# A four-layer decoder trunk on one Trainium2 core: program order and hand plan replaced by a list scheduler; layer 3's queries in 512-column products, its sinks as a score column, norm sums on GpSimd

## The chip, the core and the metric

The kernel runs on one core of one Trainium2 chip. The core has five engines that run their own instruction queues in order: PE (TensorE, matrix products), DVE (VectorE), ACT (ScalarE), POOL (GpSimd) and SP (SyncE, which here only issues DMAs). The metric is the time of one execution in device microseconds. The kernel before takes 1160.29 us (median of three runs, 1159.99 to 1162.09).

## What is computed

256 tokens of width 1024 pass through four layers, all in fp32. Cut to what matters:

```python
for i in range(4):
    a = rms_norm(h, attn_norm_g[i])
    # i % 3 == 0: differential attention (layers 1 and 4), 8 heads of 2x64, values of 128
    # i % 3 == 1: block attention, plain causal at 256 tokens (layer 2), 16 heads of 64
    # i % 3 == 2: window of 128, 16 query heads over 2 key heads, biases and sinks (layer 3)
    h = h + mixer(a) @ w_out
    u = max(rms_norm(h, mlp_norm_g[i]) @ w_up, 0)          # 1024 -> 4096
    h = h + (u * u) @ w_down
return rms_norm(h, final_norm_g)

# layer 3, one head: s are the masked scores, sink is one number per head
m = max(max(s, -1), sink)
p = exp(s - m) / (sum(exp(s - m)) + exp(sink - m))
```

In layers 1 and 4 the difference of two softmaxes is taken and its product with the values is normed again, head by head.

## The kernel before

**Numbers in two parts.** Every operand of a large product is split into a high and a low part in PE's fast fp32 format, and each product is made of three: high by high, high by low, low by high. A product of 128 weight columns with 256 tokens is written as one 512-column instruction (high weights by both token parts) and one 256-column instruction (low weights by the high part). Where the tokens are the stationary side (`proj`, `p_last`) it is three instructions of the width of the weight piece.

**Weights.** They are streamed from HBM in 193 DMAs, nearly all 1 MB pieces of 128x2048. ACT makes the high part of each piece in two halves (`whi`, L80) and DVE the low part (`wlo`, L81). Four raw pieces and three split ones fit in SBUF.

**Stages of a layer.** `proj` makes queries, keys and values (PE tiles `p_in`). The norm's factor r is not needed before these leave PSUM: the gain alone is put on the activations (`hg`), and r is a column factor at the eviction. Its sum of squares is made as squares on ACT (`sq`, L231) and sums on DVE (`acc`, L236 and L240), summed across partitions by a product with ones on PE (`p_sum`, L247), and turned into r by ten small DVE instructions (`rsqrt`, L205 to L209). Evictions then go to `qk`, `v` or `qn`, rotary terms are put on (L302 to L307), PE turns queries and keys (`p_qk`, L454), `scores` (PE `p_s`, DVE L331, ACT exponentials) and `transposed` (`p_t`) follow, the product with the values (`p_av`) gives `oo`, and the output product (`p_d`, `p_e`) adds to the residual stream `hT`. Then `up_proj` (16 groups, `p_up`) and `down_proj` (8 groups, `p_down`); in the last layer `down_out` makes the token-major `p_last` and the final norm. In the feed-forward the norm's factor is a row of 256 numbers (`p_row`, L262).

**The joint of two layers** is the place where the last group of `down_proj` is added to `hT`, its gain and square made, the sum over partitions taken and r found, while PE already runs the next layer's first `p_in` products. r has to be there when PE comes to the first `p_qk`, which stands behind 73 instructions of `p_in` in layers 2 and 4.

**What sets the order.** The program is written in the order of the work. Inside layers 1, 2 and 4 a hand-written plan (L558 to L561) says behind which half of which `proj` each block of attention goes; in layer 3 a three-deep line of heads (`step`, L436) does. The Tile framework then sets the order on each engine from this. In layer 3, queries come in four 256-column products of four heads' pairs each, and each head's sink enters as an extra exponential on ACT (`es`, L338) and an addition on DVE (`l`, L339). In layers 1 and 4 each pair of heads runs the ten-step `rsqrt` on DVE between its values and `o` (L402). PSUM's eight banks are four of `wk` (short work) and four of `acc` (sums).

## Time and profile before

| what | value |
| --- | --- |
| median of three runs | 1160.29 us |
| profiled execution | span 1158.7 us |
| instructions | 16976 |
| PE busy | 1140.8 us, 98% |
| PE weight load busy | 980.9 us, 85% |
| DVE busy | 832.8 us, 72% |
| ACT busy | 663.7 us, 57% |
| POOL busy | 11.4 us, 1% |
| DMA, mean of the span | 171 GB/s |

The profiled execution's own time is its span, 1158.7 us, and some 1.6 us lie between that and the median of the runs; a sum made against the span is carried to the median by adding 1.6. A matmul's record lasts longer than the pitch at which they follow one another, since they are pipelined, so PE's busy share cannot be read as the share of useful work. A row of a timeline gives start, length, engine, line, operation and tiles; a row of the waits gives the engine that waited, for whom, how long in all and how often.

### The profile page before, as it was taken

How to read it: one execution, taken by the hardware profiler on the slowest of the kernel's cores; microseconds unless marked ns; L12 is line 12 of the kernel's file. 1: busy time of each engine (PE TensorE's matmuls, PEld its weight loads, DVE VectorE, ACT ScalarE, POOL GpSimd, SP SyncE). 2: the span in 40 equal slices, each digit the busy share in tenths (PEclk: the TensorE clock that was granted, in tenths of full speed). 3: DMA queues.
4: the chain of work that ended last, by engine and by line, in shares of the span. 5: the costliest groups of instructions: out<-in, count | busy, mean ns of one | idle time of the engine just before them, and what ended most of it. 6: DMA issues, size and time to landing. Idle time of an engine off the chain costs nothing.

```text
span 1158.7 us, 16976 instructions
## 1 busy us (share of the span) xinstructions
PE 1140.8 (98%) x6484; PEld 980.9 (85%) x6484; DVE 832.8 (72%) x1672; ACT 663.7 (57%) x1213; POOL 11.4 (1%) x39
## 2 busy tenths in 40 slices
PE   9999999999999999999999999999999999999996
PEld 7788888888887788888899688888888889888885
DVE  7887977656676697775669798775567788777453
ACT  6876656544476666654446665654447676655341
POOL 1000000000000000000000000000000000000000
PEclk9999999999999999999999999999999999999998
DMA  9543465555544355555553245555553444554540
GB/s 330 188 145 111 164 203 193 200 185 184 180 146 146 114 178 202 199 182 186 190 213 127 73 146 190 199 193 182 185 198 132 153 151 141 194 194 163 194 169 37
DMA packets 30321, 198.66 MB, mean 171 GB/s; under 512 B 3488, under 2 KB 4640, under 8 KB 7072
## 3 DMA queue, kind: packets, MB, share of 16 engines
q1 hardware_dynamic: 29952, 197.06, 49.3%
q8 instruction: 51, 0.84, 0.3%
q10 hardware_dynamic: 288, 0.52, 0.1%
q14 instruction: 30, 0.25, 0.1%
HBM read 196.52 MB, written 1.05 MB: 171 GB/s over the span
## 4 chain that ended last, share of the span: by engine, by line
PE 89%; DVE 6%; ACT 2%; DMA 1%; issue 1%; SPq 0%; ACTq 0%
PE p_up L591 20%; PE p_in L294 15%; PE p_down L591 15%; PE p_up L592 10%; PE p_down L592 8%; PE p_last L270 2%; PE p_last L269 2%; PE p_last L271 2%; DVE wlo L81 2%; PE p_e L591 1%; PE p_t L349 1%; PE p_d L591 1%; PE p_s L269 1%; DMA raw<-in_weights 1%; PE p_av L429 1%
## 5 line engine op out<-in xcount | busy, mean ns | idle before, releaser
L81 DVE TENSOR_TENSOR wlo<-raw,whi 128x1024 fp32r<-128x1024 f32 (+1 forms) x374 | 447.3, 1209 | 203.3 <-ACT whi L80 202.8
L80 ACT ACTIVATE whi<-raw 128x1024 fp32r<-128x1024 f32 (+1 forms) x374 | 384.2, 1045 | 211.9 <-issue 109.8
L591 PE MATMUL p_up<-hg,whi 128*128 128x512 f32 x1024 | 356.8, 393 | 0.2
L592 PE MATMUL p_up<-hg,wlo 128*128 128x256 f32 x1024 | 285.2, 279 | 0.0
L591 PE MATMUL p_down<-uu,whi 128*128 128x512 f32 x768 | 266.4, 392 | 0.0
L591 PEld LDWEIGHTS p_up<-hg,whi 128*128 128x128 f32 x1024 | 191.6, 187 | 43.3 <-DVE hg L227 0.7
L592 PE MATMUL p_down<-uu,wlo 128*128 128x256 f32 x768 | 214.3, 279 | 0.0
L294 PE MATMUL p_in<-whi,hg 128*128 128x512 f32 (+1 forms) x736 | 212.5, 371 | 0.3 <-ACT whi L80 0.2
L592 PEld LDWEIGHTS p_up<-hg,wlo 128*128 128x128 f32 x1024 | 193.2, 189 | 0.4
L591 PEld LDWEIGHTS p_down<-uu,whi 128*128 128x128 f32 x768 | 143.7, 187 | 32.2
L294 PEld LDWEIGHTS p_in<-whi,hg 128*128 128x128 f32 x736 | 132.1, 188 | 23.5 <-ACT whi L80 1.3
L592 PEld LDWEIGHTS p_down<-uu,wlo 128*128 128x128 f32 x768 | 144.8, 188 | 0.0
L294 PE MATMUL p_in<-wlo,hg 128*128 128x512 f32 (+1 forms) x368 | 129.9, 368 | 0.2 <-DVE wlo L81 0.2
L664 ACT ACTIVATE uu<-u 128x512 fp32r<-128x512 f32 x64 | 40.5, 633 | 72.2 <-DVE u L662 72.2
L294 PEld LDWEIGHTS p_in<-wlo,hg 128*128 128x128 f32 x368 | 68.8, 189 | 11.7 <-DVE wlo L81 0.8
L597 ACT ACTIVATE cross<-p_up 128x256 f32<-128x256 f32 x128 | 48.2, 376 | 39.6 <-PE p_up L592 34.8
L226 ACT ACTIVATE hg<-hT,gn 128x256 fp32r<-128x256 f32 x64 | 31.7, 502 | 66.4 <-DVE hT L610 65.0
L334 ACT ACTIVATE e<-ns,nm 128x128 f32<-128x128 f32 (+1 forms) x128 | 56.9, 446 | 11.0 <-DVE nm L331 10.3
L665 DVE TENSOR_TENSOR uu<-u,uu 128x512 fp32r<-128x512 f32 x64 | 44.2, 691 | 21.8 <-ACT uu L664 21.8
L598 DVE TENSOR_TENSOR relu<-p_up,cross 128x256 f32<-128x256 f32 x128 | 53.5, 418 | 1.4 <-ACT cross L597 1.3
L271 PE MATMUL p_last<-whi,uu 128*128 128x512 f32 x128 | 49.8, 389 | 0.0
L270 PE MATMUL p_last<-wlo,uu 128*128 128x512 f32 x128 | 49.8, 389 | 0.0
(181 smaller groups left out, 1245.1 us busy)
## 6 DMA issues: line engine op xcount, KB each, us to landing
raw<-in_weights SPq DMA_DIRECT2D x181, 1024.0 KB, 4.9
raw<-in_weights SPq DMA_DIRECT2D x8, 256.0 KB, 4.5
raw<-in_weights SPq DMA_DIRECT2D x4, 512.0 KB, 8.1
hT<-in_xT SPq DMA_DIRECT2D x8, 128.0 KB, 4.3
bias<-in_swa_row SPq DMA_DIRECT2D x1, 512.0 KB, 3.5
grow<-in_fng SPq DMA_DIRECT2D x1, 512.0 KB, 3.7
out<-res ACTq DMA_DIRECT2D x2, 256.0 KB, 2.7
out<-res SPq DMA_DIRECT2D x2, 256.0 KB, 2.7
```

The lines of the kernel that those rows point to most:

```text
L80: A.activation(hi[:, s], raw[:, s], AF.Copy)
L81: V.tensor_tensor(lo[:, s], raw[:, s], f(hi[:, s]), op=OP.subtract)
L270: T.matmul(out, lh, rl, start=False, stop=False, **kw)
L271: T.matmul(out, ll, rh, start=False, stop=stop, **kw)
L294: T.matmul(out[t], n.both[k // 2][:, k % 2, x, P * t:P * t + P], r3(kb)(parts[k // kb][w])[:, k % kb, :], start=fresh, stop=k == 7 and x + ...
L334: A.activation(e[:, s], ns[:, s], AF.Exp, bias=nm[:, t:t + 1], scale=-1.0, accum_out=l[:, t:t + 1])
L591: T.matmul(r3(2)(p), hi, x, start=start, stop=False, skip_group_check=True)
L592: T.matmul(p[:, :S], lo, x[:, 0], start=False, stop=stop, skip_group_check=True)
L597: A.activation(cross, p[:, S:], AF.Copy)
L598: V.tensor_tensor(out, p[:, :S], cross, op=OP.add)
L664: A.activation(both[:, :, 0], r3(2)(u), AF.Copy)
L665: V.tensor_tensor(both[:, :, 1], r3(2)(u), f(both[:, :, 0]), op=OP.subtract)
```

## The change

The whole program is recorded as tasks (engine, cost, what must be done before) and given out by a list scheduler. PE's order is that of the scheduler, since each of its instructions is kept in program order; on DVE, ACT and POOL the framework still reorders within what the tasks allow. The large products are a chain in the old order of the weights, with places for the attention's small products set where the scheduler's costs say that they can start.

```diff
+        for t in reversed(self.tasks):
+            if t.done is not None:
+                t.due = t.done - t.cost
+            for x in t.after:
+                x.due = min(x.due, t.due - x.cost - (x.lag if x.engine != t.engine else 0.0))
...
+def urgency(task, progress):
+    if task.rank != 3:
+        return (task.rank, task.order)
+    return (0 if task.due - progress < SOON else 3, task.due)
...
+    def matmul(o, lhsT, rhs, start, stop):
+        tc.keep_in_program_order(T.matmul(o, lhsT, rhs, start=start, stop=stop, skip_group_check=True))
```

The norm's sum over partitions goes to POOL, and the factor of the tokens is then picked out of the summed rows with the identity on DVE. Only the first norm of layer 1 keeps the product with ones.

```diff
-        p = bank("wk", "p_sum")
-        for t in range(NT):
-            T.matmul(p[:, P * t:P * t + P], n.acc[:, P * t:P * t + P], ones, start=True, stop=True)
...
+                G.partition_all_reduce(self.s, self.acc[:, :S], P, bass_isa.ReduceOp.add)
...
+                V.tensor_tensor(s, s, ident[:, None, :].to_broadcast([P, NT, P]), op=OP.mult)
+                V.tensor_reduce(x, s, axis=AX.X, op=OP.add)
+                V.tensor_scalar(x, x, 1.0 / D, EPS, op0=OP.mult, op1=OP.add)
```

The small rsqrt of the head pairs (layers 1 and 4) and that of the final norm become a power on POOL:

```diff
-        rsqrt(y, ss, 2 * NT)
...
+                G.tensor_tensor(st["y"], st["ss"], minus_half, op=OP.pow)
...
-            rsqrt(r[:, o], x[:, o], 1)
...
+            a = add("POOL", 0.5, lambda: G.tensor_tensor(r[:, o], x[:, o], minus_half[:, :1], op=OP.pow), [a])
```

Layer 3's queries are two 512-column products, and the sink is written by POOL into columns on both sides of the scores, so that the exponential that makes the sum takes it in:

```diff
-            for c in range(4):
-                p = proj(n, (256, 1), False, first)
...
+        for c in ("kv", 0, 1):
+            p, last = proj(n, 256 if c == "kv" else 512)
...
-                A.activation(es, nm, AF.Exp, bias=sinks[c][0])
-                V.tensor_tensor(l, l, es, op=OP.add)
...
+                            G.tensor_copy(st["ns", c][:, 0:3 * P + 2:3 * P + 1], sinks[c].to_broadcast([P, 2]))
```

Output products of layers 2 and 3 take the form that layers 1 and 4 had (four pieces of rows, three 256-column instructions each). Evictions of `p_up`, `p_down` and additions to `hT` are made for two groups at a time, 512 columns instead of 256, with `acc` as two double banks. In the last layer, the second token block of the last piece goes in two halves of 256 columns, and the last scaling is split at column 384 between ACT and DVE.

PE's instructions by kind, before and after: `p_in` of 256 columns 240 and 48, of 512 columns 864 and 960; output products of layers 2 and 3, 128 of 512 and 128 of 256 columns, then 384 of 256; `p_last` 96 of 512 columns fewer and 192 of 256 more; `p_sum` with ones 10 and 2; `p_row` 3 and 0. All else on PE has the same columns.

**DVE at the joint of layers 1 and 2**, before (`y` is the down product's last group, `wlo` the low parts of weight pieces, `nx` and `nr` the norm's sum and factor):

```order
L598 TENSOR_TENSOR y<-p_down,cross 128x256
L81 TENSOR_TENSOR wlo_3140<-raw_2968,whi_3139 128x1024
L609 TENSOR_TENSOR y<-y,row 128x256
L610 TENSOR_TENSOR hT_70<-y,hT_70 128x256
L227 SCALAR_TENSOR_TENSOR hg_3014<-hT_70,gn,hg_3014 128x256
L236 TENSOR_TENSOR acc_3108<-acc_2925,sq 128x512
L240 TENSOR_TENSOR acc_3110<-acc_3108 128x256
L81 TENSOR_TENSOR wlo_3148<-raw_3018,whi_3147 128x1024
L249 TENSOR_SCALAR nx<-p_sum 128x2
```

and after, from the same group to the start of the rsqrt:

```order
L914 TENSOR_TENSOR y<-p_down,cross 128x512
L219 TENSOR_TENSOR wlo_2967<-raw_2838,whi_2966 128x1024
L1003 TENSOR_TENSOR y<-y,row 128x512
L1004 TENSOR_TENSOR hT_70<-y,hT_70 128x512
L219 TENSOR_TENSOR wlo_3005<-raw_2864,whi_3004 128x1024
L386 SCALAR_TENSOR_TENSOR hg_2986<-hT_70,gn,hg_2986 128x256
L404 TENSOR_TENSOR acc_2469<-acc_2469,sq 128x512
L386 SCALAR_TENSOR_TENSOR hg_2986<-hT_70,gn,hg_2986 128x256
L406 TENSOR_TENSOR acc_2469<-acc_2469 128x256
L219 TENSOR_TENSOR wlo_3005<-raw_2864,whi_3004 128x1024
L425 TENSOR_TENSOR rows<-rows,ident 128x256
L426 TENSOR_REDUCE nx<-rows 128x2
```

The low part of the layer's fourth weight piece (`wlo_3005`) now stands in front of the last gains and sums; before, only the piece ahead of it stood inside the chain. Two more halves of a low part (`wlo_3058`) stand among the small steps of the rsqrt that follow.

Behind these steps r is made, the evictions of `p_in` and the rotary steps follow, and PE's first turn (`p_qk`) waits for them. That turn stands behind 73 `p_in` instructions of the layer in both programs.

**DVE at the last eviction of layer 3's queries**, before (`qn` queries out of PSUM, `ns` the masked negative scores, `l` and `rl` the sums and their reciprocals, `e` the exponentials):

```order
L502 SCALAR_TENSOR_TENSOR qn<-p_in,nr,bias 128x2x64
L81 TENSOR_TENSOR wlo_6722<-raw_6043,whi_6721 128x1024
L331 ISA ns,nm<-p_s_6352,band,rest 128x128
L331 ISA nm 128x1
L331 ISA ns,nm<-p_s_6353,band,rest 128x256
...
L464 SCALAR_TENSOR_TENSOR qhl<-p_qk,qhl 128x512
L339 TENSOR_TENSOR l<-l,es 128x2
L302 TENSOR_TENSOR ropea<-qn,cc 128x128
L418 RECIPROCAL rl_6351<-l 128x2
```

and after:

```order
L879 SCALAR_TENSOR_TENSOR qn<-p_in,nr,bias 128x512 x2
L533 ISA ns,nm<-p_s_5940,band,rest 128x256
L533 ISA nm 128x1
L485 TENSOR_TENSOR ropea<-qn,cc 128x256
L486 TENSOR_TENSOR ropeb<-qn,nsn 128x16x8
L488 TENSOR_TENSOR ropeb<-qn,sn 128x16x8
L219 TENSOR_TENSOR wlo_5963<-raw_5729,whi_5962 128x1024
L490 TENSOR_TENSOR qn<-ropea,ropeb 128x16x16
L749 RECIPROCAL rl_6015<-l 128x2
```

The additions of the sinks' exponentials are gone, and the last eviction now holds four blocks' queries instead of two. From it to the layer's last `oo`, DVE's queue after the change holds 10 score reductions of 128 and 11 of 256 columns, 12 reciprocals with two scalings each, 6 halves of low weight parts, 2 low parts of queries and 4 `oo` of 512 columns.

**POOL from the head of the program to layer 4**, before:

```order
L135 AFFINE_SELECT causal<-causal 128x128 x2
L135 AFFINE_SELECT band<-band 128x128 x2
L137 AFFINE_SELECT band<-band 128x128
L364 MEMSET kpadh 64x2x256 x2
L364 MEMSET kpadl 64x2x256 x2
L155 MEMSET invt 128x2 x8
L159 MEMSET an_lo 128x16
```

and after, from layer 1's head pairs to layer 3's mixer (an ISA row without tiles sets up the library of the next):

```order
L693 TENSOR_TENSOR ry<-ss,minus_half 128x4 x4
L415 ISA
L415 ISA rows<-acc_1469 128x256
L575 MEMSET kpadh 64x2x256 x2
L575 MEMSET kpadl 64x2x256 x2
L415 ISA rows<-acc_2469 128x256
...
L532 COPY ns<-rest 128x2 x2
L415 ISA rows<-acc_5129 128x256
L532 COPY ns<-rest 128x2 x14
```

The sums over partitions now stand in POOL's queue, three of them at the joints of layers and four in the feed-forward stages, with the clearing of the keys' tiles and the sinks' copies around them.

1302 lines of the change are left out of this document (795 added, 507 removed).

## The prediction

> **What bounds the kernel now.** I read the page first: the shares of the engines and the chain that ended last.
>
> ```profile
> span 1158.7 us, 16976 instructions
> PE 1140.8 (98%) x6484; PEld 980.9 (85%) x6484; DVE 832.8 (72%) x1672; ACT 663.7 (57%) x1213; POOL 11.4 (1%) x39
> PE 89%; DVE 6%; ACT 2%; DMA 1%; issue 1%; SPq 0%; ACTq 0%
> ```
>
> The products bound it: 89% of the chain is PE, and DMA 1%. So the change can gain only what PE does not spend on products: the head, the tail, and waits within. To find these I read the busy time in stretches (a stretch, its length, then PE, PE's weight load, DVE, ACT and POOL busy with their counts): head and layer 1's mixer, its feed-forward, the joint into layer 2, layer 3's mixer, layer 4's mixer, and the tail.
>
> ```profile
> 0.00:48.00 48.00, 45.00 (x209) 36.27 (x210) 39.20 (x125) 35.84 (x66) 5.18 (x27) 1.00 0.74 269
> 48.00:122.00 74.00, 72.52 (x453) 63.19 (x453) 59.17 (x173) 50.15 (x128) 0.00 (x0) 1.00 0.42 144
> 122.00:298.00 176.00, 176.00 (x1021) 155.34 (x1020) 125.92 (x175) 95.83 (x140) 0.00 (x0) 1.00 0.55 190
> 298.00:323.00 25.00, 24.98 (x121) 20.44 (x121) 16.11 (x32) 10.84 (x16) 2.09 (x4) 1.00 0.51 178
> 595.00:679.00 84.00, 81.33 (x555) 68.07 (x554) 69.80 (x235) 54.97 (x146) 0.00 (x0) 1.00 0.33 112
> 856.00:968.00 112.00, 110.78 (x637) 95.28 (x635) 84.03 (x234) 72.02 (x168) 0.00 (x0) 1.00 0.44 150
> 1149.40:1158.70 9.30, 0.00 (x0) 0.00 (x0) 4.80 (x21) 2.10 (x4) 0.00 (x0) 0.61 0.30 113
> ```
>
> Outside head and tail, PE's open idle time is small: 1.5 us in layer 1 after 48 us, 2.7 in layer 3, 1.2 in layer 4. The waits name what it stood for:
>
> ```profile
> PE p_o L407 <- DVE o L402: 2.4, 6, 0.5
> PE p_d L591 <- DVE oo L433: 2.1, 5, 1.3
> PE p_qk L454 <- DVE qk L307: 1.2, 1, 1.2
> PE p_warm L129 <- POOL ones L125: 1.1, 1, 1.1
> ```
>
> But a busy PE need not be at its pitch. In the feed-forward, a timeline of PE shows what the pitch is:
>
> ```profile
> 170.13 0.28 PE L592 MATMUL p_up<-hg,wlo 128*128 128x256 f32 x1
> 170.25 0.39 PE L591 MATMUL p_up<-hg,whi 128*128 128x512 f32 x1
> 170.48 0.28 PE L592 MATMUL p_up<-hg,wlo 128*128 128x256 f32 x1
> ```
>
> A pair of 256 and 512 columns takes 170.48 - 170.13 = 0.35 us start to start, though the two records are 0.67 us long. Laying steady pitches (0.23 us for 512 columns, 0.12 for 256, 0.11 for 128) over the products of each stage, I estimate what PE really lost: some 7.3 us in layer 1 before 122 us (3.6 of it before 48 us), 2.0 in layer 2's mixer, 8.9 in layer 3's, 3.3 in layer 4's, and below 0.4 in each feed-forward. That is 23 us at most, and the tail.
>
> **Layer by layer: the products.** The counts are those of the program's order. `p_in` loses 192 of 256 columns (-23.0 us) and gains 96 of 512 (+21.8 to 22.1): -1. The output products of layers 2 and 3 lose 128 pairs at 0.35 (-44.8) and gain 384 of 256 columns at 0.12 (+46.1): +1.3. `p_last` loses 96 of 512 and gains 192 of 256: +1.0. Sums with ones fall from 20 records at some 0.11 and 6 at some 0.25 to 4: -2.8. The values' products of layer 3 come in half as many instructions, an estimated -0.5. Sum -2.0; between 0 and -3.
>
> **The tail.** From PE's last product, rows of all engines:
>
> ```profile
> 1148.95 0.39 PE L271 MATMUL p_last<-whi,uu 128*128 128x512 f32 x1
> ...
> 1149.63 0.75 DVE L698 SCALAR_TENSOR_TENSOR res<-p_last,factor,res 128x512 f32<-128x512 f32 x1
> 1150.41 0.63 ACT L700 ACTIVATE sq<-res 128x512 f32<-128x512 f32 x1 [2.24 <-DVE res L698]
> ...
> 1151.73 0.15 DVE L705 TENSOR_TENSOR fx<-fss 128x1 f32<-128x1 f32 x1
> ...
> 1154.04 0.72 ACT L709 ACTIVATE res<-res,fr 128x512 f32<-128x512 f32 x1 [2.26 <-DVE fr L209]
> ```
>
> The twelve small steps from 1151.73 to 1154.04 (2.3 us) become two on DVE (0.4) and one power on POOL. No row shows a POOL power; POOL's two longest kinds, quoted below, are 0.3 and 0.5 us, so with two changes of engine I take 0.9. Eviction and square have half the columns: -0.5 together. Gain 1.0 + 0.5 + 0.3 for the split scaling = 1.8; from 0.8 (a power of 1.5 us) to 2.5.
>
> **Layer 1 and the other mixers.** Each pair of heads in layers 1 and 4 loses ten small steps on DVE, for which the row of waits `p_o` <- DVE `o` stands (2.4 us in 6). The rotary tables get the lowest rank, so they no longer stand in front of low weight parts. What can be had is at most the 7.3 us of layer 1 and the 5.3 of layers 2 and 4; at least nothing. Between these ends, nothing in the trace chooses, so I take the middle: -3.6 and -2.6.
>
> **The joints into layers 2 and 4.** This is the place where the change lengthens a chain. Rows of PE, DVE and ACT of before in the joint into layer 2:
>
> ```profile
> 301.63 0.86 PE L294 MATMUL p_in<-whi,hg 128*128 128x512 f32 x3
> ...
> 307.45 0.69 DVE L236 TENSOR_TENSOR acc<-acc,sq 128x512 f32<-128x512 f32 x1
> 308.17 0.43 DVE L240 TENSOR_TENSOR acc<-acc 128x256 f32<-128x256 f32 x1
> 308.52 1.22 DVE L81 TENSOR_TENSOR wlo<-raw,whi 128x1024 fp32r<-128x1024 f32 x1
> 309.65 0.15 DVE L249 TENSOR_SCALAR nx<-p_sum 128x2 f32<-128x2 f32 x1
> ...
> 312.61 0.16 DVE L209 SCALAR_TENSOR_TENSOR nr<-nw,nr 128x2 f32<-128x2 f32 x1
> 314.09 1.25 ACT L574 ACTIVATE qk<-p_in,nr 128x512 f32<-128x512 f32 x2
> 315.37 0.43 DVE L302 TENSOR_TENSOR ropea<-qk,cc 128x256 f32<-128x256 f32 x1
> ...
> 316.58 1.22 DVE L81 TENSOR_TENSOR wlo<-raw,whi 128x1024 fp32r<-128x1024 f32 x1
> 318.77 1.03 PE L454 MATMUL p_qk<-ident,qk 128*128 128x128 f32 x8
> ```
>
> Count from the layer's first product, 301.63. The sums are there at 7.0, r at 11.1, rotary terms at 15.0, and PE comes to the turn only at 17.1: 2.1 us of slack. After the change, `wlo_3005` stands in front of the last gains on DVE; its raw piece's split buffers come free after the layer's first piece, 24 products at 0.2275 = 5.5. Two groups of the page and of the layer 3 window have what follows:
>
> ```profile
> L80 ACT ACTIVATE whi<-raw 128x1024 fp32r<-128x1024 f32 (+1 forms) x374 | 384.2, 1045 | 211.9 <-issue 109.8
> ```
> ```profile
> L227 DVE SCALAR_TENSOR_TENSOR hg<-hT,gn,hg 128x256 fp32r<-128x256 f32 x6 | 2.8, 479 | 0.6 <-ACT hg L226 0.6
> ```
>
> ACT's high part 1.05 and DVE's low part 1.2 give 7.75, two gains and two sums of 0.48, 0.69, 0.48 and 0.43 less some overlap 1.9, so the sums are there at 9.6. The reduction on POOL takes X. Picking out the factor is three steps of DVE, an estimated 1.0 (the 256-column row above is 0.43); the rsqrt ten steps at the tail's pitch (twelve in 2.31 us), 1.9; two halves of a low part stand among its steps, 2.4. So r is there at 14.9 + X; the eviction adds 1.25 and the rotary steps 1.3: 17.4 + X, against a turn that stands behind the same 73 products, at 17.1. PE waits X + 0.3. Behind the waiting turn stand all large products of the layer, as PE's order is fixed.
>
> No row of before shows X. These are its two longest kinds:
>
> ```profile
> L364 POOL MEMSET kpadh<- 64x512 f32 x8 | 4.2, 521 | 843.4 <-PE p_down L592 843.2
> L135 POOL TENSOR_SCALAR_AFFINE_SELECT causal<-causal 128x128 f32<-128x128 f32 x2 | 0.5, 295 | 0.0
> ```
>
> A pass over 128x256 costs by these rows 0.4 to 0.6 us; a reduction across partitions needs at least one, and its reads and writes of other partitions are not in them. I take X = 1.2, two such passes. Each joint then costs 1.5: +3.0. The lower end is 0 (the low part finds its buffer sooner); the upper is taken with X = 3, 3.3 each.
>
> [...]
>
> **Layer 3.** Rows of DVE in its mixer, grouped by shape:
>
> ```profile
> L81 DVE TENSOR_TENSOR wlo<-raw,whi 128x1024 fp32r<-128x1024 f32 x18 | 21.9, 1218 | 2.5 <-ACT whi L80 2.3
> L331 DVE CUSTOM_DVE_ANT_0 ns<-p_s,band,rest 128x256 f32<-128x256 f32 x16 | 7.4, 481 | 0.6 <-PE p_s L271 0.2
> L421 DVE TENSOR_SCALAR e<-e,rl 128x256 f32<-128x256 f32 x16 | 5.6, 348 | 0.0
> L339 DVE TENSOR_TENSOR l<-l,es 128x2 f32<-128x2 f32 x16 | 2.5, 158 | 1.3 <-ACT es L338 1.2
> ```
>
> DVE is busy 69.8 of 84 us here, and PE waits for its `oo` (2.1 us above). The sinks' additions go: 16 x 0.16 = 2.5 us and 1.3 of idle time. What counts is DVE's queue from the last eviction of queries to the last `oo`. After the change that is: evictions and rotary steps 2.9, six low halves 6.8, 10 score rows of 128 columns (0.43 with the read of the sum) and 11 of 256 (0.56), 10.5 together, twelve reciprocals with their scalings 9.5, queries 1.5, `oo` 2.8: 34 us. Behind the last `oo` stand 69 `p_d` products, 8.3 us. That is 42 to 44 us against 40.5 us of PE's own products in the stretch, so DVE decides it, by 2 to 4 us; and the joint ahead costs X + 0.3 to X + 3. Together 5 to 15 us of waits where before had 8.9. I take 11: +2.
>
> **From output product to feed-forward.** The additions to `hT` come two at a time in 512 columns, and `acc` and a low part stand ahead of the last gains on DVE (0.69 + 1.13), while PE's first up products want those gains in order, two pairs (0.7 us) for each. 0 to +1.5 at each of four places, by how much of the 1.8 is covered; I take +0.5: +2.
>
> **Sum.** -2.0 - 1.8 - 3.6 - 2.6 + 3.0 + 2.0 + 2.0 = -3.0. Against the span 1158.7 that is 1155.7, and 1.6 us more to the median of the runs: 1157.3. A measurement of this kernel can tell about 0.2%, 2.3 us, from no change.
>
> **Rivals.**
>
> A. The waits vanish: r is in time everywhere and the mixers run at PE's pitch. Then layer 1 -6, layers 2 and 4 -4.5, layer 3 -3, joints and feed-forward starts 0, products -2, tail -2.3: -17.8, 1142.5. For it: 23 us are there to be had, and DVE has over a quarter of the span free. Against: the chain of r is longer by count.
>
> B. The chain of r takes the place of the waits removed, slower than before. Place: PE's first `p_qk` of layers 2, 3 and 4. Price: with X = 3, 3.3 + 3.3 at two joints, +6 in layer 3 and +4 at the feed-forward starts, against -2.0 - 1.0 - 2.5 - 1.0 elsewhere: +10, 1170. It decides from about X = 2 on, where joints and layer 3 eat all gains. For it: only 2.1 us of slack in the joint now, all eaten before X begins. Against: POOL's rows are short.
>
> [...]
>
> D. Nothing comes of it: PE's open idle time was small, and what I count as lost at pitch is no wait but how such products run. Then -2 to +2: 1160.
>
> **How the numbers follow.** The forecast with its own range of 1152 to 1162 has 0.39, of it 0.27 faster by more than 0.2% and 0.12 within. A has 0.20, B 0.28 (of it 0.27 slower), C 0.05, D 0.08 (within). So faster 0.47, same 0.21, slower 0.32. The range leaves out C, the lower half of A and the top of B: 1142 to 1176.
>
> **What would show it.** The forecast is right if POOL's reduction (L415) takes 1 to 2 us, PE waits 1 to 2 us at the first `p_qk` of layers 2 and 4, layer 3's mixer is 82 to 86 us long, and the stretch from 0 to 122 us of before is 3 to 4 us shorter. It is wrong on the slow side if L415 is 3 us or more and its row of waits stands first, and on the fast side if no wait at `p_qk` is seen and layer 3's mixer is below 80 us.

## The result and the profile after

| | before | after |
| --- | --- | --- |
| median of four runs | 1160.37 us | 1171.30 us |
| lowest to highest | 1159.99 to 1162.09 | 1169.31 to 1173.95 |
| span of the profiled execution | 1158.7 us | 1169.2 us |

The ratio is 1.0093, with a 95% interval of 1.0077 to 1.0108. The forecast was a little faster, 1157.3 us; the kernel became slower by 0.9%, which is the sign of rival B.

The page of the kernel after, its engines and the chain that ended last:

```profile
span 1169.2 us, 16784 instructions
PE 1141.6 (98%) x6558; PEld 988.1 (85%) x6558; DVE 806.3 (69%) x1412; ACT 644.6 (55%) x1099; POOL 41.8 (4%) x71
PE 89%; DVE 7%; ACT 1%; issue 1%; POOL 1%; POOLq 0%; ACTq 0%; DVEq 0%
```

DVE lost 26.5 us of work and ACT 19.1, as the change meant; POOL gained 30.4. PE's busy time is the same within 1 us, and the span is 10.5 us longer. So the question is where PE stands, or goes slower. The waits of PE after (for whom, us in all, times, the longest):

```profile
PE p_qk L177 <- DVE qk L490: 8.2, 5, 3.3
PE p_up L174 <- DVE hg L386: 3.0, 3, 1.0
PE p_qk L177 <- DVE qn L490: 1.7, 1, 1.7
```

The waits for `o` and `oo`, 2.4 and 2.1 us before, are gone. In their place stand `p_qk` behind the rotary steps and `p_up` behind the last gains. POOL's groups show the two new operations:

```profile
L415 POOL PARTITION_ALL_REDUCE rows<-acc x7 | 15.2, 2174 | 226.0 <-DVE acc L406 226.0
L693 POOL TENSOR_TENSOR ry<-ss,minus_half 128x4 f32<-128x4 f32 x8 | 9.1, 1133 | 178.9 <-DVE ss L689 178.9
L1082 POOL TENSOR_TENSOR fr<-fx,minus_half 128x1 f32<-128x1 f32 x2 | 1.1, 551 | 164.1 <-DVE fx L1071 164.1
```

The reduction takes 2.2 us in the mean (1.79 to 2.62), a power over 128x4 1.1 us in the mean, one over 128x1 at the tail 0.55.

The stages tell where the 10.5 us are. Each is cut at PE's first product of the next one (mix: `p_in` to the first `p_up`; before, the last output products of layers 1 and 4 run into "up", so there mix and up are read together):

| | head | L1 mix, up, down | L2 mix, up, down | L3 mix, up, down | L4 mix, up, last | tail |
| --- | --- | --- | --- | --- | --- | --- |
| before | 5.76 | 115.55, 91.58, 88.75 | 115.54, 89.32, 88.75 | 83.41, 89.40, 88.75 | 111.96, 93.34, 87.24 | 9.36 |
| after | 6.21 | 114.59, 91.66, 89.92 | 119.57, 91.66, 89.92 | 82.49, 90.01, 89.70 | 115.90, 91.32, 89.20 | 7.05 |

Each profile is of one execution. The pace of PE's products and the halvings of its clock, both below, differ between profiles even in stages whose work an edit does not change: the same up stage of layer 1 is 91.66 us long here and 90.01 in the kernel with the turn set later. So a stage's length is best compared at the same pace and clock.

Windows of after (stretch, length, PE, PEld, DVE, ACT, POOL, clock, DMA): down of layer 1 and the mixers of layers 2, 3 and 4.

```profile
212.46:302.38 89.92, 89.92 (x514) 78.46 (x513) 50.10 (x54) 38.68 (x46) 2.08 (x4) 1.00 0.54 188
302.38:421.95 119.57, 115.43 (x675) 97.90 (x674) 80.64 (x201) 73.03 (x148) 2.61 (x1) 0.97 0.41 141
603.53:686.02 82.49, 76.33 (x484) 63.91 (x483) 62.34 (x183) 47.72 (x116) 6.02 (x16) 0.98 0.34 116
865.74:981.64 115.90, 111.74 (x658) 97.40 (x657) 83.53 (x199) 75.79 (x174) 6.71 (x5) 1.00 0.43 149
```

And down of layer 1 of before beside them:

```profile
212.89:301.63 88.74, 88.74 (x514) 78.24 (x513) 52.14 (x66) 39.79 (x51) 2.09 (x4) 1.00 0.55 190
```

Two things are to be seen. The mixers of layers 2 and 4 hold 4 us of idle PE each, where before had 0.0 and 1.3. And "down" has no idle time in either kernel, the same 514 records and the full clock, yet is 1.2 us longer after: PE goes slower there without waiting for anyone.

**The joint into layer 2**, rows of PE, DVE and POOL of after:

```profile
311.23 0.42 DVE L406 TENSOR_TENSOR acc<-acc 128x256 f32<-128x256 f32 x1
311.83 2.61 POOL L415 PARTITION_ALL_REDUCE rows<-acc  x1 [10.43 <-DVE acc L406]
314.47 0.42 DVE L425 TENSOR_TENSOR rows<-rows,ident 128x256 f32<-128x256 f32 x1 [1.69 <-POOL rows L415]
316.09 1.23 DVE L219 TENSOR_TENSOR wlo<-raw,whi 128x1024 fp32r<-128x1024 f32 x1
317.31 1.22 DVE L219 TENSOR_TENSOR wlo<-raw,whi 128x1024 fp32r<-128x1024 f32 x1
318.73 0.39 PE L174 MATMUL p_in<-whi,hg 128*128 128x512 f32 x1
319.41 0.16 DVE L369 SCALAR_TENSOR_TENSOR nr<-nw,nr 128x2 f32<-128x2 f32 x1
321.83 0.43 DVE L490 TENSOR_TENSOR qk<-ropea,ropeb 128x256 f32<-128x256 f32 x1
322.40 1.94 PE L177 MATMUL p_qk<-ident,qk 128*128 128x128 f32 x8 [3.28 <-DVE qk L490]
```

Counted from the layer's first product at 302.38: the sums end at 9.3, the reduction stands from 9.5 to 12.1, two halves of a low part (2.4 us) stand among the steps of the rsqrt, r is there at 17.2, the rotary steps at 19.9. PE comes to the turn at 16.7 and stands for 3.28 us. In the wait the clock falls. Windows of after around it:

```profile
318.00:320.00 2.00, 1.12 (x5) 0.58 (x4) 1.40 (x7) 0.33 (x1) 0.00 (x0) 1.00 0.45 57
320.00:322.00 2.00, 0.00 (x0) 0.00 (x0) 1.00 (x4) 2.00 (x4) 0.00 (x0) 0.77 0.80 336
324.00:325.00 1.00, 1.00 (x5) 0.81 (x4) 1.00 (x2) 0.72 (x3) 0.00 (x0) 0.50 0.00 0
327.00:328.00 1.00, 1.00 (x4) 0.72 (x4) 0.00 (x1) 0.00 (x0) 0.00 (x0) 0.54 1.02 434
328.00:330.00 2.00, 2.00 (x10) 1.64 (x9) 0.00 (x0) 0.00 (x0) 0.00 (x0) 1.00 0.32 135
```

PE runs at 0.50 from the end of its wait at 322.4 to about 327.9. In these 5.5 us stand 8 products of 128 columns and 9 of 512, which at the steady pitches (0.11 and 0.2275 us) take 2.9: some 2.6 us are lost on top of the 3.28. At the joint into layer 4 the wait is as long, and the clock stays at 1.00:

```profile
882.07 0.39 PE L174 MATMUL p_in<-whi,hg 128*128 128x512 f32 x1
885.75 1.07 PE L177 MATMUL p_qk<-ident,qk 128*128 128x128 f32 x8 [3.29 <-DVE qk L490]
```

Five of the kernels below keep both waits at 3.3 us (rows by products, all tiles shifted, score tile padded, gains ahead of the sums, power off POOL). In their profiles the clock halves in or just behind the first wait in four, for 3.4 us, and at the second in three, for 3.4 or 6.8 us. So the wait is steady, and what the clock adds to it differs from profile to profile.

**The pace of the pairs.** A timeline of PE in layer 1's up stage of after:

```profile
149.92 0.40 PE L174 MATMUL p_up<-hg,whi 128*128 128x512 f32 x1
150.16 0.28 PE L174 MATMUL p_up<-hg,wlo 128*128 128x256 f32 x1
150.27 0.40 PE L174 MATMUL p_up<-hg,whi 128*128 128x512 f32 x1
```

and the same in layer 3's:

```profile
719.88 0.39 PE L174 MATMUL p_up<-hg,whi 128*128 128x512 f32 x1
720.11 0.28 PE L174 MATMUL p_up<-hg,wlo 128*128 128x256 f32 x1
720.22 0.39 PE L174 MATMUL p_up<-hg,whi 128*128 128x512 f32 x1
```

A 512-column product takes 0.24 us start to start in the one and 0.23 in the other. Over all pairs of a stage the mean from start to start is 0.3532 us in layers 1, 2 and 4 and 0.3467 in layer 3; in "down" 0.3513, 0.3513 and 0.3504. Before, it was 0.3467 in every down stage, and at most 0.3475 in an up stage. The granted clock is 1.00 in all of them. A stage has 256 pairs, so the slow pace costs 256 x 0.0065 = 1.7 us.

### The profile page after: what moved, and what is told of

Read it like the earlier page. It is cut to its first block, busy times and chain, and to the rows that moved or that the text cites. A ratio compares the mean times of both kernels' runs of the same rounds, so it can differ in the third digit from the quotient of the medians.

```text
span 1169.2 us, 16784 instructions
## 1 busy us (share of the span) xinstructions
PE 1141.6 (98%) x6558; PEld 988.1 (85%) x6558; DVE 806.3 (69%) x1412; ACT 644.6 (55%) x1099; POOL 41.8 (4%) x71
## 4 chain that ended last, share of the span: by engine, by line
PE 89%; DVE 7%; ACT 1%; issue 1%; POOL 1%; POOLq 0%; ACTq 0%; DVEq 0%
PE p_up L174 30%; PE p_down L174 23%; PE p_in L174 15%; PE p_last L174 7%; PE p_d L174 6%; DVE wlo L219 3%; PE p_s L174 3%; PE p_av L174 2%; PE p_qk L177 1%; PE p_t L177 1%; ACT whi L215 1%; DVE hg L386 1%; POOL rows L415 1%; DVE hT L937 1%; PE p_warm L174 0%
## 5 line engine op out<-in xcount | busy, mean ns | idle before, releaser
L174 PE MATMUL p_in<-whi,hg 128*128 128x512 f32 (+1 forms) x672 | 189.5, 395 | 3.2 <-ACT whi L215 1.6
L174 PEld LDWEIGHTS p_in<-whi,hg 128*128 128x128 f32 x672 | 124.7, 192 | 27.7 <-ACT whi L215 2.0
L174 PE MATMUL p_in<-wlo,hg 128*128 128x512 f32 (+1 forms) x336 | 106.0, 393 | 0.3 <-DVE wlo L219 0.3
L174 PE MATMUL p_d<-oo,whi 128*128 128x256 f32 x512 | 94.7, 285 | 0.0
L174 PE MATMUL p_last<-whi,uu 128*128 128x256 f32 (+1 forms) x320 | 82.6, 348 | 0.0
L174 PEld LDWEIGHTS p_d<-oo,whi 128*128 128x128 f32 x512 | 78.4, 188 | 1.3 <-issue 0.9
L174 PEld LDWEIGHTS p_in<-wlo,hg 128*128 128x128 f32 x336 | 62.7, 190 | 13.6 <-DVE wlo L219 1.2
L540 ACT ACTIVATE e<-ns,nm 128x128 f32<-128x128 f32 (+3 forms) x128 | 57.1, 449 | 30.3 <-DVE nm L533 30.1
L174 PE MATMUL p_d<-oo,wlo 128*128 128x256 f32 x256 | 71.6, 280 | 0.0
L174 PEld LDWEIGHTS p_last<-whi,uu 128*128 128x128 f32 x320 | 55.6, 188 | 8.3
```

What stands on the lines that cost most here:

```text
L174: tc.keep_in_program_order(T.matmul(o, lhsT, rhs, start=start, stop=stop, skip_group_check=True))
L540: A.activation(st["e"][:, c, s], st["ns", c][:, s], AF.Exp, bias=st["nm", c][:, t:t + 1], scale=-1.0, accum_out=sums_of(c)[:, t:t + 1])
```

## The experiments

Three theories stood at the start, and each could explain part of the 10.5 us. **The joint**: the chain of r, with POOL's reduction on it, is longer than the place that the scheduler gave it in PE's order. **The rows**: the reductions that replaced the feed-forward's `p_row` products change how PE runs. **The place of the tiles**: the score tile `ns` is now 386 columns wide instead of 384, so the tiles allocated behind it move by 64 bytes against the weights (by the addresses in the program). Ratios below are against before on the same chip, with the 95% interval.

### The factor at the joints by products again

```diff
-        r = n.factor(False) if i else None
+        r = n.factor(True) if i else None
...
-            a = dve(2, done, [a])
+            a = dve(1350 if self.joint else 2, done, [a])
```

> The norm sums at the three joints of layers are made by products with ones on PE instead of the reduction on POOL, at a place in PE's order where the sums are ready; the first turn (p_qk) stays behind about as many p_in products (75 instead of 73 in layers 2 and 4, 89 instead of 86 in layer 3). Theory of the long chain (the joint's chain of r is too long for PE's fixed order): r comes some 3 us earlier, PE's 3.3 us waits at p_qk in layers 2 and 4 fall below 0.5 us, the halved clock behind layer 2's joint goes, and the time falls by 6 to 9 us, to about 1163. Theory of the feed-forward pitch (most of the loss is that pairs of up and down products follow each other at 0.351 to 0.353 us instead of 0.347): 7 to 8 us of the loss stay, the up and down stages keep their lengths within 0.3 us, and the time stays above 1160.4. Both can hold.

Measured: 1163.89 us, 1.0020 [1.0010, 1.0031]. The mixer of layer 2 in this kernel:

```profile
303.79:418.14 114.35, 113.08 (x678) 96.29 (x677) 79.92 (x199) 72.90 (x148) 0.00 (x0) 1.00 0.43 148
```

It falls from 119.57 to 114.35, that of layer 4 to 114.01 and that of layer 3 to 81.41. The longest wait for `qk` is 1.1 us, where less than 0.5 was expected, and the clock is at 1.00 in layers 2 and 4. So the joint is most of the loss. It doesn't tell whether POOL's 2.6 us are at fault or the place of the turn; the next does.

### The reduction kept, the turn set later

Only the scheduler's price for POOL's reduction at a joint is changed, from 3 to 7 us. The chip does the same work; PE's first turn moves behind 85 `p_in` products of layers 2 and 4 instead of 73, and behind 106 instead of 86 in layer 3.

```diff
-            return add("POOL", 3.0, do, [self.last], rank=rank)
+            return add("POOL", cost, do, [self.last], rank=rank)
...
-            return x, dve(512, do, [self.row(rank)], 3, rank=rank)
+            return x, dve(512, do, [self.row(rank, 7.0)], 3, rank=rank)
```

> The scheduler is told that the joint's reduction takes 7 us instead of 3; the work is the same, but PE's first turn now stands behind 85 p_in products instead of 73 in layers 2 and 4 and behind 106 instead of 86 in layer 3. Theory of the long chain: r comes as late as before, but PE has 2.7 us more work in front of the turn; the waits at p_qk fall from 3.3 to about 0.6 us, no halved clock follows, and the time falls by 5 to 8 us, less what later scores cost in layer 3 (0 to 3 us). If instead the POOL reduction slows the work beside it, or the turn's place does not matter, the time stays within 1.5 us of 1171.

Measured: 1160.96 us, 1.0001 [0.9992, 1.0011]. Mixers of layers 2, 3 and 4:

```profile
300.25:413.80 113.55, 112.54 (x675) 95.87 (x674) 80.25 (x201) 73.29 (x148) 2.61 (x1) 1.00 0.43 149
595.37:675.98 80.61, 76.68 (x485) 64.00 (x483) 63.04 (x184) 47.95 (x116) 5.23 (x17) 0.98 0.35 118
858.16:971.60 113.44, 112.06 (x658) 97.38 (x657) 83.32 (x199) 76.12 (x174) 6.71 (x5) 1.00 0.44 152
```

and the row of waits:

```profile
PE p_qk L177 <- DVE qk L490: 1.9, 4, 0.6
```

One number in the scheduler takes back 0.9%. The first `p_qk` of layer 2 starts 20.01 us after the layer's first product, as in after (20.02): the chain of r is as long as it was, and the reduction still takes 2.61 us. But PE does 12 more products meanwhile (12 x 0.23 = 2.7 us) and waits 0.6 at most, and the clock is 1.00 over the mixer where it was 0.97. The mixers lose 6.0, 1.9 and 2.5 us. So it isn't the reduction's length by itself that made the loss: the turn stood 3.3 us too early for the chain, and either a shorter chain (the run before) or a later turn takes most of the loss back.

### The feed-forward's rows by products again

```diff
+                matmul(self.s, ones, self.acc[:, :S], True, True)
...
-                s = n.row()
+                s = n.row_by_products()
```

> Only the feed-forward's sum goes back to a product with ones on PE, behind the second group of up products. If the pitch of the feed-forward is a state of PE's queue that a short foreign product puts right (in the kernel before the pitch went from 0.353 to 0.347 us at p_row in layer 3), up stages of layers 1 and 2 get 1.3 us shorter, with down stages up to 1.2 us each, and the time falls by 3 to 6 us. If the pitch comes from where tiles lie or from the double PSUM banks, up and down stages stay within 0.3 us of the changed kernel's 91.7 and 89.9 us, and the time changes by less than 1 us. The theory of the long chain at the joints expects no change here either.

Measured: 1169.62 us, 1.0081 [1.0054, 1.0108], against after's 1.0093: no difference that can be told. Up of layers 1 to 3 is 90.4 to 90.7; the pairs are quick from the start in layer 1, and begin slow and turn quick behind the product in layers 2 and 3. But in three of the four kernels below that have the same product and the padded tile, pairs turn from quick to slow behind it in some stage. So the product does not by itself give the quick pace; it is a place at which the pace can change, either way. What taking it out of before does is shown further below.

### All tiles shifted

```diff
+    cst.tile([P, 40], F32, name="shift")
```

160 bytes ahead of the large tiles.

> A tile of 160 bytes that nothing uses shifts every large SBUF tile, so that they lie to 256 bytes as in the kernel before; nothing else changes. If the place of the tiles sets the pitch of the feed-forward, pairs go to 0.347 us in all up and down stages and the time falls by 7 to 8 us. If not, every stage stays within 0.3 us and the time within 1 us of 1171.

Measured: 1171.26 us, 1.0084 [1.0062, 1.0106]. "Down" stays at 89.70 to 89.81, so its extra length doesn't come from the absolute place of the tiles. Up of layers 1 and 2 is quick in this profile, 90.01 each, which neither expectation had. But the profiled execution is the fastest of four (1167.58, the others 1169.77 to 1173.15), and the kernel with the turn set later, whose tiles lie as in after, has a quick up in layer 1 too. So that the shift made these stages quick isn't shown, and the median didn't move.

### The score tile padded

```diff
-                        st["ns", c] = sb.tile([P, 3 * P + 2], F32, tag="ns", name="ns", bufs=2)
+                        st["ns", c] = sb.tile([P, 512], F32, tag="ns", name="ns", bufs=2)
```

> The score tiles ns, which the two sink columns made 1544 bytes wide, are padded to 2048; nothing else changes. In the kernel before every large tile lies 224 bytes behind a multiple of 512; in the changed kernel the weight parts lie at 320 and the tiles behind ns (most of uu) at 384. Theory of the displaced tiles: down pairs then follow at 0.347 us instead of 0.350 to 0.351 in all three down stages (88.7 to 88.8 us instead of 89.7 to 89.9), -1.0 to -1.2 each, and p_last gets up to 1 us shorter; time -3 to -4.5. Against it: the pitch of the down stages stays above 0.350 and the time within 1.5 us of 1171. The up stages read hg, which lies at 320 already, so neither says anything of them.

Measured: 1169.55 us, 1.0073 [1.0058, 1.0088]: less than the 3 us expected, and against after's 1.0093 no difference that can be told; in this profile the clock also halves for 6.8 us in layer 4's mixer. "Down" is 90.46, 88.75 and 88.75: with the tile padded, here and in all seven later kernels that have it so, a down stage has either before's pace to the hundredth or the slow one (pairs of 0.3467 or 0.3533), and none of the 0.3504 to 0.3513 between. So the values between come from the place of the tiles against one another, and the slow pace doesn't; at the slow pace, the padded stage is even the longer one (90.46 against 89.92).

### Before with the wide score tile, and nothing else

The two columns are allocated and not used.

```diff
-            ns = sb.tile([P, 3 * P], F32, tag="ns", name="ns", bufs=2)
+            ns = sb.tile([P, 3 * P + 2], F32, tag="ns", name="ns", bufs=2)
```

> Another part alone, in the kernel before: the score tiles are two columns wider and nothing uses these, so that most of uu lies 64 bytes off the weight parts within 512. Theory of the displaced tiles: the three down stages go from 88.75 us to 89.7 or more with pairs at 0.350 to 0.351, the up stages stay, and the time rises by 2.5 to 4. Against it: down stages stay at 88.75 and the time within 1 us.

Measured: 1164.35 us, 1.0030 [1.0017, 1.0042]. Up and down of layer 1:

```profile
122.07:213.51 91.44, 91.44 (x532) 80.79 (x533) 76.12 (x113) 56.62 (x89) 0.00 (x0) 1.00 0.55 186
213.51:303.16 89.65, 89.65 (x515) 78.33 (x513) 52.14 (x66) 40.05 (x51) 2.08 (x4) 1.00 0.55 189
```

Eight unused bytes per row cost 3.6 us. Each down stage is 0.9 us longer (pairs of 0.3501 for 0.3467), the last layer's last stage 1.4, up unchanged. This shows the displaced tiles alone, without the change: 3 x 0.9 + 1.4 = 4.1 us by the stages, 3.6 by the medians. In after the last stage has less of it (0.5 by the padded kernel, 88.73 against 89.20).

### Before with the rows on POOL

The sum lands in a tile `rows` of SBUF instead of a PSUM bank, and `dynamic_dma_scratch_size` is set to 15360 beside it.

```diff
-        T.matmul(p[:, :S], ones, n.acc, start=True, stop=True)
+        G.partition_all_reduce(p, n.acc, P, bass_isa.ReduceOp.add)
```

> One part of the change alone, in the kernel before: the feed-forward's sum goes from the product p_row on PE to the reduction on POOL; order, joints and tiles (224 bytes behind a multiple of 512) stay. If the product behind the second up group is what puts PE's pace at 0.347 us in every stage of that kernel, up and down stages now fall to 0.353 in some stages, 1.7 us each for a stage, the runs scatter by 5 us or more and the median rises by 3 to 9 us. If the pace comes from elsewhere, all stages stay at 0.347 and the time stays within 1 us of before.

Measured: 1163.39 us, 1.0015 [1.0005, 1.0025]. The ten times lie in two bunches, 1159.8 to 1160.5 (three) and 1163.2 to 1164.6 (seven); the profiled execution is one of the first bunch, with every stage at the quick pace. The 22 times of before on that chip lie between 1159.91 and 1161.95, so taking the product out did make this kernel slower in most executions, by a little less than the 3 us expected. The step between the bunches, 3.5 us, is about that of two stages at the slow pace, such as an up stage with its down (1.7 each). That the pace is what makes it is argued from the times; no profile of the second bunch was taken.

### The last gains ahead of the sums

The sums of the norm lose their rank over the last gains on DVE.

```diff
-                    n.sum(j, [adds[j]])
+                    n.sum(j, [adds[j]], rank=3)
```

> The feed-forward's norm sums get the rank of the gains, so that on DVE the copy into acc no longer stands ahead of the last gains (one low part still does). If the wait of PE's first up products is DVE's order there, it falls from 1.0 to about 0.3 us in three layers: time -1.5 to -2.5. If those waits are covered otherwise: within 1 us.

Measured: 1169.89 us, 1.0078 [1.0063, 1.0093]. The wait of `p_up` falls from 3.0 to 1.8 us, its longest from 1.0 to 0.6; up of layers 1 to 3 is 0.4 us shorter each. The wait does shrink, by 1.2 us in all; the median's ratio can't be told from after's 1.0093.

### The head pairs' power off POOL

Layers 1 and 4 do the ten-step rsqrt on DVE again.

```diff
-                G.tensor_tensor(st["y"], st["ss"], minus_half, op=OP.pow)
+                rsqrt(st["y"], st["ss"], 2 * NT)
```

> The head pairs' power on POOL is the ten-step rsqrt on DVE again. If the power gave what my forecast booked for it (a part of -3.6 and -2.6 in the mixers of layers 1 and 4), those two mixers get 1 to 3 us longer and the time rises by 2 to 5 us. If a power of 1.1 us on POOL with two changes of engine is no shorter for PE than ten steps of 0.19 us, the time stays within 1 us of 1171.

Measured: 1173.06 us, 1.0101 [1.0083, 1.0118], against after's 1.0093 no difference that can be told. Layer 1's mixer is the same (114.64 against 114.59). Layer 4's is 1.75 us longer (117.65), but it holds a stretch at half clock, which after's does not:

```profile
886.15:892.98 6.83, 6.04 (x19) 5.10 (x20) 4.86 (x7) 3.00 (x5) 0.00 (x0) 0.50 0.56 202
```

PE is busy for 6.04 us of it, so up to 3.0 us are lost to the clock, and PE's waits for `qk` in that mixer are 3.3 us where after has 4.1. Without the halved clock it would be no longer than after's. So no gain from POOL's power shows in either mixer.

### Joint and tiles mended, with rows by products: four kernels on the pace

The first has the turn set later, the padded tile and the rows by products, the last layer's factor among them:

```diff
-            return x, dve(512, do, [self.row(rank)], 3, rank=rank)
+            return x, dve(512, do, [self.row(rank, cost)], 3, rank=rank)
...
-                        st["ns", c] = sb.tile([P, 3 * P + 2], F32, tag="ns", name="ns", bufs=2)
+                        st["ns", c] = sb.tile([P, 512], F32, tag="ns", name="ns", bufs=2)
...
-                s = n.row()
+                s = n.row_by_products()
...
-                x, a = n.column()
+                x, a = n.column_by_products([main[0]])
```

> Three mends at once: PE's first turn behind 85 p_in products (told 7 us for the joint's reduction), the feed-forward's norm sums as products on PE behind the second up group (in layer 4 too), and the padded ns. If the joints (-10.3 by the run that moved the turn), the up pitch reset by a foreign product (up to -1.4 in each of four up stages) and the displaced tiles (-3 to -4.5) are three separate causes, they add up: 1150 to 1156, faster than the kernel before. If the pitch is only chance of a run, the time stays at 1159 to 1162, as with the moved turn alone.

Measured: 1160.19 us, 1.0001 [0.9979, 1.0022]. Its ten times go from 1154.87 to 1167.74, where 13 runs of before on that chip go from 1160.07 to 1162.26; its profile has all stages slow, up of layer 2 from the row's product on. So the three gains did not add up to the 1150 to 1156 expected. The second is the first with all tiles shifted, so that they stand at before's place within 512 bytes:

```diff
+    cst.tile([P, 104], F32, name="shift")
```

> As the run with the three mends (turn's place told 7 us, sums as products, padded ns), and every large SBUF tile moved by 416 bytes, so that all lie 224 bytes behind a multiple of 512, as in the kernel before. That kernel's up and down pairs were at 0.347 us in all stages, those of the three-mends run at 0.353. If the place of the tiles within 512 bytes decides which of the two paces PE falls into, all stages are at 0.347, the time is 1150 to 1154 and the runs lie within 3 us of each other. If not, stages at 0.347 and at 0.353 stay mixed, with a median of 1157 to 1163 and a spread of 8 us or more.

Measured: 1165.81 us, 1.0033 [1.0012, 1.0054], slow and quick stages mixed; the place within 512 bytes isn't what decides. The third is the first with the sums of `p_up` in single banks, as before had them:

```diff
-                        st["p"] = two_banks("p_up")
+                        st["p"] = [bank("p_up") for _ in range(2)]
```

> As the run with the three mends, with the up products in two single PSUM banks of wk (banks 0 to 3, as in the kernel before) instead of a double bank of acc (4 to 7), and their evictions 256 columns at a time. If the banks decide PE's pace, up and down stages are at 0.347 us and the time is 1150 to 1155. If not, both paces stay mixed and the median lies at 1157 to 1163.

Measured: 1164.39 us, 1.0024 [1.0004, 1.0044], mixed; banks don't decide either. The fourth is the first with PE's instructions free for the framework to reorder:

```diff
-        tc.keep_in_program_order(T.matmul(o, lhsT, rhs, start=start, stop=stop, skip_group_check=True))
+        T.matmul(o, lhsT, rhs, start=start, stop=stop, skip_group_check=True)
```

> As the run with the three mends, without the call that keeps PE's instructions in program order; the framework then moves a few of them (first turns stay behind 85 and 106 products). If the kept order decides PE's pace, up and down stages are at 0.347 us and the time is 1150 to 1156. If not, both paces stay mixed, with a median of 1157 to 1163.

Measured: 1154.76 us, 0.9940 [0.9920, 0.9960]. The median is the one expected if the kept order decides the pace, but the paces are mixed as in the three before it, so that isn't the reason. Layer 3's mixer is 77.50, against 80.54 in the first of the four, which has 3.4 us at half clock in it and the other none. No edit here restored the quick pace everywhere. Layer 4's up stage was slow in every kernel made from after, and quick in every one made from before (0.3532 us a pair in after, at most 0.3475 in before).

The profiles show two things more of the pace. In all 18 of them an up stage's pace is set within its first 32 pairs, and past these it changes at the row's product alone. And with tiles at their places (before, before with the rows on POOL, and the eight kernels with the padded tile) each down stage has the pace at which the up ahead of it ended, 30 times out of 30. So a slow up goes with a slow down behind it, 3.4 us together.

### Joint, tiles and gains mended, rows on POOL

The change as it was, with the price of 7, the padded tile and the gains first, by three of the edits above:

```diff
+            return x, dve(512, do, [self.row(rank, cost)], 3, rank=rank)
...
+                        st["ns", c] = sb.tile([P, 512], F32, tag="ns", name="ns", bufs=2)
...
+                    n.sum(j, [adds[j]], rank=3)
```

> The changed kernel with the turn's place told 7 us, the padded ns and the gains ahead of the sums on DVE; all sums past layer 1's first stay on POOL. By adding what these gave alone (-10.3, -1.7, -1.4) the median is 1157 to 1160. If the products in the feed-forward are needed to bring PE back to its quick pace, it stays at 1160 or above.

Measured: 1154.60 us, 0.9952 [0.9936, 0.9969]. Mixer and up of layer 2, and the mixer of layer 3:

```profile
299.05:412.97 113.92, 112.93 (x674) 96.25 (x673) 80.34 (x201) 73.40 (x148) 2.61 (x1) 1.00 0.43 149
412.97:502.47 89.50, 89.08 (x514) 78.25 (x513) 73.85 (x92) 52.12 (x71) 1.79 (x1) 1.00 0.55 187
591.22:670.52 79.30, 75.36 (x484) 63.06 (x483) 63.02 (x183) 48.09 (x116) 4.99 (x16) 1.00 0.36 121
```

The median is 2.4 us below the 1157 expected at best. The profiled execution, 1151.35 us, is the fastest of the four; up and down of layers 1 to 3 are all quick in it, without the row's product, and the clock is at 1.00 in every mixer. With these three mended, the change is 0.5% faster than before: the gains were there. With PE's order left free as well (the edit of `keep_in_program_order` above):

> The version with the turn's place told 7 us, padded ns and gains first, without the call that keeps PE's order. In the three-mends version this made layer 3's mixer 3.1 us shorter (77.5 after 80.6). If that was the order and not chance, it is 1151 to 1154 here with layer 3's mixer below 78.5. If it was chance of the pace, the median stays at 1154 to 1157 and layer 3's mixer at 79 or more.

Measured: 1152.97 us, 0.9945 [0.9927, 0.9963]; layer 3's mixer is 77.25, 2.05 us shorter than above, both at full clock, as expected of the free order. It has the lowest median of all versions tried, and beats both kernels; from the one above it can't be told by the intervals. In its profile (1156.3 us) every up and down stage is at the slow pace.

### The queries in 256 columns again

The same kernel as 0.9952, with layer 3's queries in four products of 256.

```diff
-        for c in ("kv", 0, 1):
-            p, last = proj(n, 256 if c == "kv" else 512)
+        for c in ("kv", 0, 1, 2, 3):
+            p, last = proj(n, 256)
```

> The version with the turn's place told 7 us, padded ns and gains first, with layer 3's queries in four 256-column products again. By PE's pitches the 512-column form saves 23.0 - 21.8 = 1.2 us, and half as many evictions and rotary steps some DVE time: layer 3's mixer gets 1 to 3 us longer than 79.3. If the later start of the last four blocks (one eviction for four blocks instead of two) costs what the products save, it stays within 0.7 us.

Measured: 1162.69 us, 1.0016 [1.0006, 1.0026]. Layer 3's mixer:

```profile
596.51:680.50 83.99, 76.67 (x580) 69.62 (x579) 64.17 (x196) 48.39 (x117) 7.18 (x17) 0.98 0.35 124
```

It is 4.7 us longer than with 512 columns (79.30), where 1 to 3 were expected. Up to 1.6 of these are the clock, which is halved near the end of this mixer and nowhere in the other:

```profile
673.12:676.54 3.42, 3.14 (x14) 3.14 (x15) 0.23 (x1) 0.00 (x0) 0.00 (x0) 0.50 0.81 280
```

So the wide queries are worth some 3 us at the same clock; whether they also keep the clock up isn't shown. The two profiled executions are 13.0 us apart, of which 6.4 lie in feed-forward stages at the slow pace and 2.1 in layer 1's mixer, which holds another halved clock. With the narrow queries PE waits for `oo` again (1.2 and 1.0 us) and 2.4 us for an eviction of queries.

## Why the prediction was wrong

The terms as booked, and as the stages of after have them:

| term | booked | measured | how |
| --- | --- | --- | --- |
| joints of layers 2 and 4 | +3.0 | +9.2 | waits 3.28 + 3.29, half clock 2.6 |
| pace of the feed-forward | not booked | +9.2 | up of 1, 2, 4 at 1.65 each; downs 1.2 + 1.2 + 0.9; last 2.0 less the 1.0 of its products |
| starts of the feed-forward | +2.0 | +3.0 | the row of `p_up` |
| layer 1 | -3.6 | -3.1 | head, mix and up -0.4, less pace 1.65 and start 1.0 |
| layers 2 and 4, rest | -2.6 | -5.2 | mix and up +6.4 and +1.9, less wait, clock, pace and start |
| layer 3 | +2.0 | -1.3 | mix and up -0.3, less start 1.0 |
| tail | -1.8 | -2.3 | 9.36 to 7.05 |
| products of the last stage | +1.0 | +1.0 | kept as booked, not measured apart |
| other products | -3.0 | in the layers' rows | |

The measured column adds up to 10.5; that of the booked to -3.0. What is "measured" here is a share worked out from the stages of one profiled execution (1170.98 us; the four lie between 1169.31 and 1173.95), and a stretch at half clock in layer 3, up to 1.7 us, is in that layer's term; the pace's 1.65 is up of layer 1 after (91.66) less the same stage at the quick pace in the kernel with the turn set later (90.01).

**The joints: the step that failed.** Its arithmetic held. The sums were booked at 9.6 and came at 9.3, r at 14.9 + X, the turn's data at 17.4 + X, and PE's wait at X + 0.3. With the measured X of 2.61 that is a wait of 2.9, and 3.28 came. What failed is "I take X = 1.2, two such passes": the rows behind the guess are of other operations, a clearing (0.52 us) and a mask (0.30 us), and the reduction takes 1.79 to 2.62 us. The upper bound of 3 was the right row to stand on, or the whole range between had to carry the chance. And what can follow a wait of 3 us was not asked: the clock halved at one of the two (0.50 for 5.5 us behind it), and 2.6 of the 9.2 us there are no wait. The kernel with the turn set later shows that even X = 2.6 costs PE at most 0.6 us a turn where the order leaves it room.

**The pace: the step that wasn't there.** The prediction took 0.35 us for a pair and the same columns for the same time. Two hundredths of that, 0.0065 us a pair, over the 256 pairs of a stage and up to seven stages come to as much as the joints. The trace of before had a sign of it: its stages are at the quick pace but for the first 32 pairs of layer 3's up, which run at 0.353 us until the row's product at 689.97 us. A part has its cause shown, the displaced tiles: 0.9 us in each down stage of before with the wide score tile. For the slow up stages, what sets the pace stays open: the place within 512 bytes, the banks, PE's kept order and the row's product were each put back to what they are in before, and none gave the quick pace everywhere. The three slow up stages of after, 5 us in the table, are therefore unexplained, and other profiles have them in other layers.

**Layer 3: the wrong sign.** "DVE decides it" took 11 us of waits where 8.9 were. That 11 doesn't follow from its own terms: 2 to 4 and X + 0.3 to X + 3 come to 3.5 to 8.2 at the X of 1.2 booked elsewhere, not to 5 to 15, and 3.5 to 8.2 is a gain. The mixer fell by 0.9, with 1.9 us in it that the later turn took away, and the queries in 512 columns are worth some 3 at the same clock. In after, PE waits for no `oo` at all, and in layer 3 for scores or values only 2.2 us. The queue counted there, 34 us behind the last eviction, didn't bind; why it didn't wasn't tested.

**Layer 1, layers 2 and 4, the tail: about right, partly by luck.** The middle between nothing and all came out near in layer 1 (-3.1, though the stretch itself is only 0.4 us shorter, since pace and start take it back), and better in layers 2 and 4 together with their products (-5.2 against -2.6 and about half of -3.0). The middle was taken because nothing chose between the ends, so its coming out near is luck; and POOL's power, one of the reasons given for these gains, shows no share in either mixer. In the products, the sums with ones come to 3.3 by the counts and prices given there, not 2.8, which would make the forecast half a us lower. The tail gained 2.3 instead of 1.8, as the power took less than the 0.9 booked. Rows of after at its end, from PE's last product:

```profile
1161.88 0.28 PE L174 MATMUL p_last<-whi,uu 128*128 128x256 f32 x1
...
1164.49 0.55 POOL L1082 TENSOR_TENSOR fr<-fx,minus_half 128x1 f32<-128x1 f32 x1 [2.07 <-DVE fx L1071]
1165.08 0.61 ACT L1074 ACTIVATE last<-last,fr 128x384 f32<-128x384 f32 x1 [1.04 <-POOL fr L1082]
```

The power takes 0.55 us, and 0.59 from its start to the scaling's, where 0.9 was booked.

**The rivals.** B came true at its place and its price: X near 3, the first `p_qk` of layers 2 and 4, 3.3 us each. Its point of decision, X of about 2, lies below the 2.6 measured, but no run tried another X. Its total of 1170 against 1171.3 is partly luck: its +6 in layer 3 didn't come, and the pace, which no rival had, stood in for it. The measured time lies inside the whole range of 1142 to 1176, in the part that was B's. C, which the chances give 0.05, had the reduction slow by itself and falls: over 256 columns it takes 2.2 us in the mean. A and D fall with the waits at `p_qk`. The sign named for the slow side was half right: the row of waits stood first, but at X of 2.6, not 3 or more.

## What to carry to other kernels

Where a program's order is planned from a table of costs, a new operation's price has to be that of its whole chain to the waiting engine, its neighbours' queues among it; here one number, 3 or 7 us, decided 0.9%, with the same work on the chip. Eight unused bytes a row in one tile moved the tiles behind it by 64 bytes and cost before 3.6 us, so look at the stages that the change does not touch, and compare their length to the hundredth of a us before giving the whole difference to a wait. And a cost that no row shows is better given by its bounds and the point from which it decides than by a guess in the middle: here that point was 2 us by rival B's count, and the guess stood below it.

## What the runs showed of the hardware

- POOL's reduction over all partitions of 128x256 takes 1.79 to 2.62 us; a power on POOL 0.55 us for 128x1 at the tail and 0.71 in layer 4, and 1.01 us for 128x4 in most cases, with one of 1.93.
- Of two waits of PE, 3.28 and 3.29 us, one was followed by 5.5 us of products at a granted clock of 0.50, the other by none. The clock also halved behind a shorter one: layer 3 of after has a wait of 1.58 us for `hg` near its start, and from 1.7 us behind its end the clock is halved for about 3.4 us. PE's row, and windows of the same place:

```profile
609.58 1.02 PE L174 MATMUL p_in<-whi,hg 128*128 128x256 f32 x4 [1.58 <-ACT hg L383]
```

```profile
610.00:611.00 1.00, 0.98 (x8) 0.90 (x8) 0.97 (x3) 0.45 (x1) 0.00 (x0) 1.00 1.00 426
612.00:613.00 1.00, 1.00 (x4) 0.81 (x3) 0.00 (x0) 1.00 (x2) 1.00 (x1) 0.50 0.00 0
615.00:616.00 1.00, 1.00 (x6) 0.80 (x5) 1.00 (x2) 0.00 (x0) 0.00 (x0) 1.00 0.00 0
```

  So the length of a wait alone does not tell whether the clock falls behind it.
- Pairs of a 512- and a 256-column product run at 0.3467 or at 0.3533 us a pair, at a granted clock of 1.00, over whole stages. What sets the pace was not found; once set in the first pairs of an up stage, it held, but for changes at the row's product, through the down stage (30 of 30 with the tiles at their places).
- A score tile wider by 8 bytes a row, unused, lengthened four stages of before by 0.9 to 1.4 us each (1.0030 [1.0017, 1.0042]).
